# A two-layer decoder trunk: rounded halves for layer 0's gate, one weight chunk and 24 scalings between engines, first sums in pairs, and a new list of the order

## The chip, the cores and the metric

The kernel runs on one core of a Trainium2 chip, in one launch. The metric is the device time in microseconds. The five engines that the profile names are PE (TensorE), DVE (VectorE), ACT (ScalarE), POOL (GpSimd) and SP (SyncE, which here only asks for transfers).

## The reference, cut to what matters

Two layers act on 256 tokens of width 1024. Each normalises, scales and shifts by a conditioning vector, mixes, and adds the gated result. Layer 0 ("even") runs sliding-window attention with sinks (8 heads) beside a three-branch sparse attention (8 heads); layer 1 ("odd") runs block-sparse attention with 16 heads.

```python
def reference(x, c, w_ada, b_ada, norm_g, w_in_even, ...):
    c_act = jax.nn.silu(c)
    for layer in range(2):
        ada = jnp.einsum('bd,de->be', c_act, w_ada[layer]) + b_ada[layer]
        shift, scale, gate = jnp.split(ada, 3, axis=-1)      # 1024 each
        h = rms_norm(x, norm_g[layer]) * (1.0 + scale[:, None, :]) + shift[:, None, :]
        y = even_mixer(h, ...) if layer == 0 else odd_mixer(h, ...)
        x = x + gate[:, None, :] * y
    return rms_norm(x, final_g)

def even_mixer(h, w_in, w_out, ...):
    proj = jnp.einsum('bsd,de->bse', h, w_in)
    ...
    oa = swa_sink_attention(qa, ka, va, sinks, cos, sin) * jax.nn.silu(za)
    ob = nsa_attention(...) * jax.nn.silu(zb)
    return jnp.einsum('bse,ed->bsd', jnp.concatenate([oa, ob], axis=-1), w_out)
```

The products of activations and weights are wanted in float32 precision.

## The kernel before, in words

**Recording and issuing.** The program does not call the engines. A `Plan` records each operation with a number in order of recording and the numbers that it depends on; the line that finally calls an engine is line 244 for all of them, which is why the profile names L244 everywhere and why its rows are told apart by tiles. `issue()` emits the operations in the order of a literal list, `ORDER` (lines 37 to 154), in which every operation must stand behind those it depends on. Each engine executes its own operations in that order, so a wait of one holds up all behind it on its engine. SP's queue asks for the transfers in list order too.

**Float32 as rounded halves.** A matmul of float32 takes two passes in the trace. Projections therefore split both sides: `split` has ScalarE round a tile (`whi<-raw`, the CAST) and VectorE subtract (`wlo<-raw,whi`), and `mm3` multiplies hi x hi, hi x lo, lo x hi. `hhi`/`hlo` are the two halves of the layer's input, `ghi`/`glo` those of the gated mixer output. There are five `raw` buffers for weights, four `whi` and four `wlo`.

**The start.** x (`xs`) is loaded and normalised while layer 0's shift and scale columns arrive. These are sums over the 1024 rows of `w_ada`, weighted by silu(c) (`cz`). `START` (line 24) gives four groups (columns per group in blocks of 128, and `d`, how many of the eight row blocks VectorE sums itself). `first_ada` (691) asks for the first group's shift and scale columns in five transfers to `qT` and `gate`; `start_ada` asks for the later groups, and `start_row` (759) for the projection's weight rows. `start_sums` (714) sums with narrow matmuls of 32 columns of the array, four column groups q at a time (q = 0, 1 are shift, q = 2, 3 scale for two-block groups), copies the result (`asb<-ps_m`), transposes it, and adds the bias into `shs`. `start_prep` makes `hhi`/`hlo` from `bigA` and `shs`; `start_mm` accumulates the projection row block by row block. Warm-up matmuls (`ps_o<-ones`) fill the time before.

**The even layer.** `attn_four` (573) handles two pairs of heads: scores, one reduction with masks, an Exp with a sum, a reciprocal `rc`, a scaling of each probability tile by `rc` (128x128 for t=0, 128x256 for t=1), transposes and copies. `ON_ACT` (line 30) names the scalings that ScalarE does; the others are VectorE's. The tiles lie in `late` and `bigA`. It is called six times.

**Conditioning sums between.** `jobs` (1072) holds what is filled in between attention steps: layer 0's gate, then layer 1's shift and scale in two halves g=0 and g=4. `ada_wide` loads two row blocks at a time into `raw`; VectorE accumulates them into `acc` (one instruction of 128x1024 per row block). `SS_PE` (line 27) says how many of the four such chunks TensorE sums instead, straight from `raw`, in `ada_shift_scale`: for each row block four matmuls of 32 columns by 256. `ada_gate` (463) sums `acc` over the partitions with a matrix of ones; `GATE_R` (line 25) says for which layer it splits `acc` into rounded halves first (`whi<-acc`, `wlo<-acc,whi`) instead of multiplying in float32.

**Between the layers and at the end.** `out_proj` multiplies by `w_out`; `add_scaled` (378) multiplies by the gate, adds to `xs` and takes sums of squares into `parts`; GpSimd raises them to the power -0.5; then the rows are normalised, transposed and shifted into layer 1's `hhi`/`hlo`. The end of layer 1 does the same with the final norm; `LAST` (line 29) cuts the output into pieces for ScalarE ("a"), VectorE ("v") and a fused one ("f"), each with a transfer of its own.

Of the kernel before, what the change touches and what calls it, by code (L numbers as in the profile page):

```python
# [24 lines left out]
GATE_R = (0, 1)  # L25
HV = 4
SS_PE = {0: 0, 4: 2}
SPL = (1024, 1024, 512, 512)
LAST = ((("a", 0, 384), ("v", 384, 1024)), (("a", 0, 192), ("a", 192, 384), ("f", 768, 1024), ("v", 384, 768)))
ON_ACT = ((0, 0, 1), (0, 1, 1), (1, 0, 1), (1, 1, 1))  # L30
# [225 lines left out]
def tile_trunk(  # L256
# [23 lines left out]
    plan = Plan(tc.nc)  # L280
# [433 lines left out]
    def start_sums(g, n, d, w):  # L714
# [9 lines left out]
        terms = []  # L724
# [7 lines left out]
        ids = []  # L732
# [11 lines left out]
        for o in range(0, len(ids), 4):  # L744
            plan.group(ids[o : o + 4])
# [640 lines left out]
```

## Time and profile before

| | before |
|---|---|
| time, median of three runs | 294.93 us (294.6 to 295.61) |
| profiled execution, time | 295.04 us |
| profiled execution, span | 293.3 us |
| granted TensorE clock, mean | 0.995 |
| busy: TensorE, VectorE, ScalarE, GpSimd | 285.4, 252.8, 188.5, 8.1 us |
| moved by DMA | 71.72 MB |

The span runs from the first to the last instruction; the execution's own time is 1.74 us longer. In rows of instructions the first number is the start in us from the beginning of the span, the second the duration in us; then come the engine, the operation, output and inputs by the program's names, shape, and a count where equal neighbours are put together. In rows of groups, "x24 | 30.6, 1276" means 24 instructions, 30.6 us together, 1276 ns each. A bracket shows how long the engine was idle before and what ended that.

### The profile page before, as it was taken

Reading aid. Unit: us, or ns where it says so; the run is one execution under the profiler, and the core shown is the slowest. Engines: PE = TensorE matmul, PEld = TensorE weight load, DVE = VectorE, ACT = ScalarE, POOL = GpSimd, SP = SyncE. Lnnn points to the kernel's source line nnn. Section 1 sums busy time; section 2 is a strip of 40 time slices with the busy share of each in tenths; the row PEclk is TensorE's granted clock in tenths of the full one; section 3 lists DMA queues with packets and bytes.
Section 4 is the critical chain, followed back from the end, with each engine's and each line's share of the span. In section 5 each row is a group of like instructions: output and inputs, shape, how many; then the busy total and the mean of one; then the engine's idle time right before and its main releaser. Section 6 shows DMA issues by size and latency. Waiting matters only on the chain.

```text
span 293.3 us, 6197 instructions
## 1 busy us (share of the span) xinstructions
PE 285.4 (97%) x2293; PEld 246.6 (84%) x2293; DVE 252.8 (86%) x629; ACT 188.5 (64%) x480; POOL 8.1 (3%) x33
## 2 busy tenths in 40 slices
PE   8999999999999999999999999999999999999991
PEld 8888788897897888777767899998899999887891
DVE  0497797999999999999889759779978999899884
ACT  4456256895998899994457863366658368584531
POOL 3000000000000000000020000000000000000021
PEclk9999999999999999999999999999999999999998
DMA  7999999999969942769986954569489709502003
GB/s 262 381 365 380 384 380 349 344 349 322 389 233 359 351 147 74 249 234 332 333 256 206 349 167 135 191 242 283 146 258 291 244 0 335 205 36 72 1 3 142
DMA packets 48431, 71.72 MB, mean 245 GB/s; under 512 B 2490, under 2 KB 33938, under 8 KB 48402
## 3 DMA queue, kind: packets, MB, share of 16 engines
q1 hardware_dynamic: 47906, 70.93, 70.6%
q8 instruction: 18, 0.29, 0.4%
q10 hardware_dynamic: 496, 0.41, 0.4%
q14 instruction: 11, 0.09, 0.1%
HBM read 70.28 MB, written 1.05 MB: 243 GB/s over the span
## 4 chain that ended last, share of the span: by engine, by line
PE 82%; DMA 11%; DVE 1%; ACT 1%; issue 1%; POOL 1%; POOLq 0%; DVEq 0%; ACTq 0%
PE ps_pj L244 53%; PE ps_s L244 10%; PE ps_o L244 7%; PE ps_pt L244 7%; PE ps_m L244 5%; DMA gate<-in_w_ada_dram 3%; DMA late<-in_w_ada_dram 3%; DMA raw<-in_w_in_even_dram 3%; DMA qT<-in_w_ada_dram 2%; DMA xs<-in_x_dram 1%; DVE wlo L244 1%; ACT t L244 1%; ACT whi L244 1%; POOL parts L244 1%; DVE t L244 0%
## 5 line engine op out<-in xcount | busy, mean ns | idle before, releaser
L244 ACT CAST whi<-raw 128x512 fp32r<-128x512 f32 (+2 forms) x116 | 71.8, 658 | 27.1 <-PE ps_pj L244 16.5
L244 DVE TENSOR_TENSOR wlo<-raw,whi 128x512 fp32r<-128x512 f32 (+2 forms) x100 | 71.3, 740 | 7.3 <-ACT whi L244 6.6
L244 PE MATMUL ps_pj<-hlo,whi 128*128 128x256 f32 x256 | 70.0, 288 | 0.0
L244 PE MATMUL ps_pj<-hhi,whi 128*128 128x256 f32 x256 | 69.9, 289 | 0.0
L244 PE MATMUL ps_pj<-hhi,wlo 128*128 128x256 f32 x256 | 68.3, 284 | 0.0
L244 PEld LDWEIGHTS ps_pj<-hhi,whi 128*128 128x128 f32 x256 | 46.7, 188 | 1.6 <-issue 0.7
L244 PEld LDWEIGHTS ps_pj<-hlo,whi 128*128 128x128 f32 x256 | 47.1, 189 | 0.8 <-issue 0.7
L244 PEld LDWEIGHTS ps_pj<-hhi,wlo 128*128 128x128 f32 x256 | 46.7, 189 | 0.3
L244 ACT ACTIVATE late<-late,mn 128x128 f32<-128x128 f32 (+1 forms) x58 | 26.0, 450 | 9.2 <-DVE mn L244 9.1
L244 DVE SCALAR_TENSOR_TENSOR acc<-raw,cz,acc 128x1024 f32<-128x1024 f32 x24 | 30.6, 1276 | 0.1
L244 PE MATMUL ps_pj<-whi,hlo 128*128 128x512 f32 (+2 forms) x72 | 25.6, 373 | 0.0
L244 PE MATMUL ps_pj<-wlo,hhi 128*128 128x512 f32 (+2 forms) x72 | 25.5, 372 | 0.0
L244 DVE SCALAR_TENSOR_TENSOR wlo<-raw,whi 128x512 fp32r<-128x512 f32 x32 | 21.1, 686 | 4.5 <-ACT whi L244 4.4
L244 PE MATMUL ps_pj<-whi,hhi 128*128 128x512 f32 (+2 forms) x72 | 24.8, 373 | 0.0
L244 PE MATMUL ps_pj<-wlo,ghi 128*128 128x512 f32 (+1 forms) x56 | 20.6, 371 | 0.0
L244 PE MATMUL ps_pj<-whi,ghi 128*128 128x512 f32 (+1 forms) x56 | 20.6, 371 | 0.0
L244 PE MATMUL ps_pj<-whi,glo 128*128 128x512 f32 (+1 forms) x56 | 20.4, 367 | 0.0
L244 PE MATMUL ps_pt<-ta,late 128*128 128x128 f32 x87 | 19.6, 275 | 0.0
L244 ACT COPY late<-ps_pt 128x384 f32<-128x384 f32 (+1 forms) x29 | 14.0, 483 | 7.9 <-PE ps_pt L244 7.6
L244 PEld LDWEIGHTS ps_pj<-whi,hhi 128*128 128x128 f32 x72 | 13.4, 188 | 2.5 <-ACT hhi L244 0.7
L244 PEld LDWEIGHTS ps_pj<-whi,hlo 128*128 128x128 f32 x72 | 13.6, 188 | 2.0 <-issue 0.2
L244 PEld LDWEIGHTS ps_pj<-wlo,hhi 128*128 128x128 f32 x72 | 13.4, 189 | 1.6
(243 smaller groups left out, 591.0 us busy)
## 6 DMA issues: line engine op xcount, KB each, us to landing
raw<-in_w_in_odd_dram SPq DMA_DIRECT2D x16, 1024.0 KB, 5.7
raw<-in_w_ada_dram SPq DMA_DIRECT2D x8, 1024.0 KB, 8.3
raw<-in_w_ada_dram SPq DMA_DIRECT2D x16, 512.0 KB, 6.3
raw<-in_w_in_even_dram SPq DMA_DIRECT2D x5, 1024.0 KB, 7.9
raw<-in_w_in_even_dram SPq DMA_DIRECT2D x7, 652.0 KB, 7.6
late<-in_w_ada_dram SPq DMA_DIRECT2D x16, 256.0 KB, 6.8
raw<-in_w_out_even_dram SPq DMA_DIRECT2D x4, 1024.0 KB, 5.8
raw<-in_w_out_odd_dram SPq DMA_DIRECT2D x4, 1024.0 KB, 8.7
```

The source lines that it names most:

```text
L244: self.ops.append(dict(key=eng.key, deps=deps, fn=lambda: getattr(real, name)(*args, **kw)))
```

## The change

Four small edits and a new order:

1. `GATE_R`: layer 0's gate is summed in rounded halves too. Two float32 matmuls become four of rounded numbers, and a cast on ScalarE and a subtraction on VectorE of 128x1024 are added.
2. `SS_PE`: in the second half of layer 1's shift and scale, TensorE sums one chunk from `raw` instead of two. Eight matmuls go; VectorE gets two accumulations of 128x1024.
3. `ON_ACT`: all eight scalings of an `attn_four` call are ScalarE's; the four of t=0, 24 in all, leave VectorE.
4. `start_sums`: in the first group (`d` = 0) the column groups are issued two at a time, so the shift's sums and the scale's are separate bursts.
5. `ORDER`: a new list for the whole kernel, with 3000 numbers instead of 3002. In it the queue of SP asks, behind x, for scale 87 and 88, shift 85, scale 89, shift 86, then for row 91 (before: 85, 86, 87, 88, 89, 90). On TensorE the first sums of the scale half come first.

```diff
-GATE_R = (0, 1)
+GATE_R = (1, 1)
...
-SS_PE = {0: 0, 4: 2}
+SS_PE = {0: 0, 4: 1}
...
-ON_ACT = ((0, 0, 1), (0, 1, 1), (1, 0, 1), (1, 1, 1))
+ON_ACT = tuple((n, i, t) for n in range(2) for i in range(2) for t in range(2))
...
 ORDER = [int(i) for i in """
...
         ids = []
-        for m in range(max(len(tq) for tq in terms)):
-            for q, tq in enumerate(terms):
-                if m < len(tq):
+        size = 4 if d else 2
+        for o in range(0, 4, size):
+            for m in range(max(len(tq) for tq in terms)):
+                for q in range(o, o + size):
+                    tq = terms[q]
+                    if m >= len(tq):
+                        continue
                     ids.append(T.matmul(
...
-        for o in range(0, len(ids), 4):
-            plan.group(ids[o : o + 4])
+        for o in range(0, len(ids), size):
+            plan.group(ids[o : o + size])
```

Of the new order the prediction uses these places. On ScalarE, the cast of row 0's columns 512 to 1024 (`whi<-raw`) stands ahead of the first `asb<-ps_m` copy; before, behind it. On VectorE, between the layers, one subtraction `wlo<-raw,whi` moves from behind the normalised row of tokens 0 to 127 to ahead of it, and the add to `xs` of tokens 128 to 255 moves ahead of both `t<-ps_pj,shs` pieces. At the end, the 128x640 output scaling of tokens 0 to 127 moves behind the last reduction. The small transfers of the second layer's rows are asked for earlier, the gate's bias later.

232 rows, old and new, of the table ORDER are left out of this document.

## The prediction

> **What bounds the kernel now.** I read the page's totals, its slices and its chain first, to see which engine sets the end.
>
> ```profile
> span 293.3 us, 6197 instructions
> PE 285.4 (97%) x2293; PEld 246.6 (84%) x2293; DVE 252.8 (86%) x629; ACT 188.5 (64%) x480; POOL 8.1 (3%) x33
> ...
> PE   8999999999999999999999999999999999999991
> ...
> GB/s 262 381 365 380 384 380 349 344 349 322 389 233 359 351 147 74 249 234 332 333 256 206 349 167 135 191 242 283 146 258 291 244 0 335 205 36 72 1 3 142
> ...
> PE 82%; DMA 11%; DVE 1%; ACT 1%; issue 1%; POOL 1%; POOLq 0%; DVEq 0%; ACTq 0%
> ```
>
> TensorE is busy for 285.4 of 293.3 us, and 82% of the chain that ended last is its matmuls. The 11% of DMA is the start; the chain's longest pieces and TensorE's list of waits say where it lies.
>
> ```profile
> 4.16 7.62 DMA gate<-in_w_ada_dram
> 11.79 7.51 DMA late<-in_w_ada_dram
> 19.32 7.42 DMA raw<-in_w_in_even_dram
> 26.75 6.09 DMA qT<-in_w_ada_dram
> ...
> PE ps_m L244 <- DMA qT<-in_w_ada_dram: 0.5, 1, 0.5
> ```
>
> From 4.16 to 32.84 us the transfers lead: the first matmuls of the projection run as fast as rows and layer 0's shift/scale columns land. At about 32.8 us TensorE waits 0.5 us for the last of them, and nowhere later does that list name a wait. So behind 33 us a microsecond is gained only by taking work from TensorE, and lost by whatever makes it wait; ahead of 33 us a short delay of TensorE costs nothing as long as the transfers end no later. The third region is the tail behind the last matmul, where the last sums, the final norm and the output's transfers stand in a row.
>
> VectorE and ScalarE over the even layer's attention, in the windows from 70 to 140 and from 100 to 130 us (columns: window, length, PE, PEld, DVE, ACT, POOL, clock, DMA share, GB/s):
>
> ```profile
> 70.00:140.00 70.00, 70.00 (x605) 55.69 (x601) 69.03 (x217) 60.16 (x180) 0.00 (x0) 1.00 0.76 266
> 100.00:130.00 30.00, 30.00 (x226) 23.19 (x224) 29.89 (x95) 28.30 (x80) 0.00 (x0) 1.00 0.52 177
> ```
>
> VectorE is full (69.03 of 70) and TensorE still does not wait for it. ScalarE has 9.84 us free over the whole, but only 1.70 in the middle 30.
>
> **Part 1, layer 0's gate in rounded halves.** The two sums over partitions and their neighbours on TensorE, and the same job as layer 1 does it already:
>
> ```profile
> 100.85 1.02 PE L244 MATMUL ps_m<-acc,ones 128*128 128x512 f32 x2
> 101.80 1.08 PE L244 MATMUL ps_o<-bigA,vb 128*64 128x256 f32 x9
> ...
> 103.74 1.02 PE L244 MATMUL ps_m<-acc,ones 128*128 128x512 f32 x2
> 104.70 0.71 PE L244 MATMUL ps_s<-late,qT 64*128 64x128 f32 x6
> ...
> L244 ACT CAST whi<-acc x1: 1049/1049/1049, 247.4 to 247.4; 128x1024 fp32r<-128x1024 f32 x1
> L244 DVE TENSOR_TENSOR wlo<-acc,whi x1: 1218/1218/1218, 248.6 to 248.6; 128x1024 fp32r<-128x1024 f32 x1
> ...
> 149.16 0.40 PE L244 MATMUL ps_s<-whi,ghi 128*128 128x512 f32 x1
> ...
> 149.63 0.40 PE L244 MATMUL ps_s<-whi,glo 128*128 128x512 f32 x1
> ```
>
> From start to start the old sums hold TensorE 0.95 + 0.96 = 1.91 us. A matmul of rounded numbers of the same width starts 0.235 us after the last (149.16 to 149.63 is two steps), so the four new ones take 0.94. **Gain 0.97 us**, all on the path. The price is 1.05 us of ScalarE and 1.22 of VectorE ahead of the sums; the gate is read by the output projection's adds (one stands at 151.02 below), so its longer way alone delays nobody. What is queued behind the two instructions matters, and comes under part 3.
>
> **Part 2, one weight chunk of layer 1's shift and scale from TensorE to VectorE.** The sums lie between the layers, and so does the chain that they fill:
>
> ```profile
> 150.42 0.69 DVE L244 TENSOR_TENSOR wlo<-raw,whi 128x512 fp32r<-128x512 f32 x1
> 151.02 0.68 DVE L244 TENSOR_TENSOR t<-ps_s,gate 128x512 f32<-128x512 f32 x1
> 151.71 1.91 PE L244 MATMUL ps_m<-raw,cz 128*32 128x256 f32 x32
> 152.54 0.40 DVE L244 TENSOR_SCALAR t<-ps_pj,shs 128x128 f32<-128x128 f32 x1
> 153.03 0.41 ACT L244 CAST hhi<-t 128x256 fp32r<-128x256 f32 x1 [1.26 <-DVE t L244]
> 153.55 0.50 PE L244 MATMUL ps_pj<-whi,hhi 128*128 128x512 f32 x1
> ...
> L244 DVE SCALAR_TENSOR_TENSOR acc<-raw,cz,acc 128x1024 f32<-128x1024 f32 x24 | 30.6, 1276 | 0.1
> ```
>
> The 32 quarter matmuls hold TensorE from 151.71 to 153.55, 1.84 us; half of them go, 0.92 us. But they were filler: the next matmul reads the cast that ends at 153.44, so at the old timing the gap would simply show. What moves the cast is VectorE's new order. The subtraction that stood at 150.42, ahead of t=1's multiply by the gate, now stands ahead of the normalised row, in a stretch where VectorE waits for GpSimd's power. The multiply can then start when its bank is complete, at about 150.75 instead of 151.02; the two h pieces and the cast come as much sooner, though the add is now ahead of both of them. I therefore take **0.27 of 0.92 as gained** (ends: 0 and 0.92). The VectorE price is 2 x 1.28 = 2.55 us, somewhere before 140 us.
>
> **Part 3, 24 scalings from VectorE to ScalarE.** The t=0 pieces and their nearest kin on ScalarE (first rows: minimum/median/maximum in ns between 70 and 140 us):
>
> ```profile
> L244 DVE TENSOR_SCALAR late<-late,rc x15: 254/279/281, 75.1 to 128.3; 128x128 f32<-128x128 f32 x15
> L244 DVE TENSOR_SCALAR bigA<-bigA,rc x9: 274/279/286, 92.9 to 132.6; 128x128 f32<-128x128 f32 x9
> ...
> L244 ACT ACTIVATE late<-late,mn 128x128 f32<-128x128 f32 x29 | 11.5, 396 | 3.5 <-DVE mn L244 3.5
> ...
> L244 ACT CAST whi<-raw 128x512 fp32r<-128x512 f32 x92 | 53.3, 619 | 22.2 <-PE ps_pj L244 14.2 <-issue 3.2 <-DMA raw<-in_w_in_even_dram 2.5
> ...
> 150.65 1.12 ACT L244 CAST whi<-raw 128x512 fp32r<-128x512 f32 x2
> ```
>
> VectorE loses 24 x 0.279 = 6.7 us and gets 1.22 + 2.55 = 3.8, so it goes from 69.03 to 66.1 of 70. ScalarE pays at most 0.396 each, as for an Exp of this shape (9.5 us); two casts in a row take 1.12 where two alone take 1.24, so in a train the price is about 0.28 (6.7). With the gate's cast ScalarE stands at 67.9 to 70.7 of 70 us. Relief of VectorE buys nothing, since TensorE waits for it nowhere here. On ScalarE the weight casts and the copies of transposed probabilities, both read by TensorE, queue behind each added scaling. Cover is the slack that VectorE had while equally full: TensorE did not wait then. I take nothing for it; the ends are 0 and the price of the first rival.
>
> The Trainium skill, "ScalarE: Activation LUTs", section "What ACT_TABLE_LOAD costs", gives an ACTIVATE with one pointer operand 280 ns + 0.833 ns per column and takes off about 93 ns back to back: by that an estimate of 294 ns for each, 7.1 us in all, and ScalarE at 68.3 of 70. That is the lower end of the two above; the trace's 1.12 us for two casts agrees with an overlap.
>
> **Part 4, the first sums in pairs, and the new first transfers.** The start of the projection:
>
> ```profile
> 11.05 1.18 PE L244 MATMUL ps_m<-qT,cz 128*32 128x128 f32 x34
> ...
> 13.10 0.27 ACT L244 COPY asb<-ps_m 128x128 f32<-128x128 f32 x1 [3.83 <-PE ps_m L244]
> 13.26 0.62 ACT L244 CAST whi<-raw 128x512 fp32r<-128x512 f32 x1
> 14.74 0.47 PE L244 MATMUL ps_s<-whi,hhi 128*128 128x512 f32 x1
> ```
>
> Two column groups at a time instead of four let a quarter's sums start when its half has landed, at up to twice the PE time of these 64 instructions; they run while TensorE waits for rows, so I cost the pairs at nothing (up to 1.2 us if that cover were gone, the length of the burst at 11.05 once more). The new list asks the queue for the scale half's chunks first, with the shift half between them. On ScalarE it also puts a weight cast of row 0 ahead of the copy `asb`, whose row is asked for behind all ada chunks: the copy then starts after landing and cast, about 0.4 us later, and so does the first matmul. The same bytes end the start at about 32.8 us, and the 0.5 us wait there absorbs 0.4. The tiny row transfers, asked for earlier, add a few KB to that queue, and the gate's bias, asked later, is needed only with the gate's sums. **Start 0** (ends: -0.5, that wait gone, and +1.2).
>
> **Part 5, the tail.** Order on VectorE and the output's transfers:
>
> ```profile
> 285.84 0.55 DVE L244 TENSOR_SCALAR t<-xs,parts 128x640 f32<-128x640 f32 x1
> 286.43 3.81 SPq L244 DMA_DIRECT2D out_dram<-t  x3
> 288.38 0.55 POOL L244 TENSOR_TENSOR parts<-parts,expo 128x1 f32<-128x1 f32 x1 [1.93 <-DVE parts L244]
> 288.96 0.42 DVE L244 TENSOR_SCALAR t<-xs,parts 128x384 f32<-128x384 f32 x1 [0.67 <-POOL parts L244]
> ```
>
> The 128x640 scaling of tokens 0 to 127 stands at 285.84 and its 320 KB are asked for at 286.43, ahead of the last 512 KB. In the new order it stands behind the last reduction, in the 0.67 us in which VectorE waits for GpSimd's power: no VectorE time is lost on the path (0.55 fits in 0.67), but the 320 KB are asked for at about 288.9 and share the way with the last 512 KB. At the 380 GB/s of the best slices of the start they alone take 0.84 us; I take **+0.5** (ends 0 and +0.9), since about half fits into the stretch before the last pieces are asked for.
>
> **The rest of the list.** Most of each engine's order changes; a common order holds only 1248 of TensorE's 1910 instructions, 245 of VectorE's 545 and 179 of ScalarE's 398. Reordering takes no TensorE time by itself; I cost it at 0, with -0.5 to +1.5 as ends.
>
> **Sum.** 295.04 us (the profiled execution; 0.11 above the median of the runs, 294.93) - 0.97 - 0.27 + 0 + 0.5 = 294.30, or 294.2 against the median. I write 294.2. What a measurement here can tell from no change is 0.3%, 0.88 us, so this is within it, near its lower edge.
>
> **Rivals.** *ScalarE becomes the bound (slower).* Place: 100 to 130 us, where 13 of the 24 scalings lay (10 on `late`, 3 on `bigA`, with the rest around them). 28.30 + 13 x 0.28 to 0.40 + 1.05 is 33.0 to 34.6 in 30 us, so 3.0 to 4.6 us of casts must have been moved out. If half of that becomes TensorE's wait it is +1.5 to +2.3: 295.7 to 296.5. It decides from about 1.6 us of wait. For it: ScalarE at 28.30 of 30 already. Against: VectorE stood at 29.89 and nobody waited. *All TensorE time is kept (faster).* The chain between the layers gives way by the whole 0.92, and the tail's transfer is hidden: 295.04 - 0.97 - 0.92 = 293.15, and 292.65 if the wait at 32.8 us goes too. For it: every edit takes from a full engine. Against: the cast at 153.03. *Nothing comes of it:* the gate's saving meets a late operand soon after, the shift/scale saving is lost, the tail takes the rest: 294.9. *The start is uncovered:* sums in pairs at twice the time and the late cast delay everything, +1.2 on the forecast: 295.4 and up.
>
> **How the numbers follow.** Forecast 0.36 (a third of it beyond 0.88 us faster), all kept 0.25, ScalarE 0.24, nothing 0.10, start 0.05 (three fifths of it slower). So faster 0.25 + 0.12 = 0.37, same 0.24 + 0.10 + 0.02 = 0.36, slower 0.24 + 0.03 = 0.27. The forecast's own range is 293.6 to 294.9; the whole one, 292.6 to 296.3, leaves out the far ends of the first two rivals, about 0.2.
>
> **What would show it.** TensorE's busy time down by near 1.9 us; four matmuls of the gate 0.235 apart; TensorE's list of waits with an entry for the cast between the layers of 0.4 to 0.7 us (0 for the second rival) and none for ScalarE between 70 and 140 us (the first rival: over 1.5 us there); the first projection matmul near 15.1 us; the last matmul 1.2 us earlier and the tail behind it 0.5 us longer. The prediction is wrong if TensorE stands still anywhere else behind 33 us.

## The result: slower by 3.2 us, and the profile after

| | before | after |
|---|---|---|
| median of the runs (four each) | 294.88 us (294.6 to 295.61) | 298.06 us (297.8 to 298.43) |
| profiled execution | 295.04 us | 298.43 us |
| span, granted clock | 293.3 us, 0.995 | 296.7 us, 0.994 |

The ratio after to before is 1.0105 (95% interval 1.0082 to 1.0128). In this and the runs below, two executions that lie far outside all others (566 us in new_cast, 1586 us of the kernel before) are left out. The forecast was 294.2 with a range to 296.3: the time lies outside, past the upper end of the first rival too (296.5).

The page of after: totals, TensorE's slices, the chain's shares; then TensorE's list of waits (us in total, times, longest).

```profile
span 296.7 us, 6148 instructions
PE 286.3 (96%) x2277; PEld 247.4 (83%) x2277; DVE 251.7 (85%) x608; ACT 194.9 (66%) x505; POOL 9.1 (3%) x33
...
PE   8999999999999998999999999999999999999990
...
PE 63%; DVE 17%; DMA 10%; ACT 4%; issue 3%; POOL 1%; POOLq 0%; DVEq 0%; ACTq 0%; SPq 0%
```

```profile
PE ps_pt L244 <- ACT t L244: 1.0, 1, 1.0
PE ps_pj L244 <- ACT hhi L244: 0.5, 1, 0.5
PE ps_pt L244 <- ACT hhi L244: 0.4, 1, 0.4
PE ps_pj L244 <- DVE t L244: 0.3, 1, 0.3
```

The chunk's sixteen records are gone from TensorE (2293 to 2277) and the gate's four hold it for 1.36 us instead of 1.91, and yet it is busy 0.9 us longer. A TensorE without gaps reads as busy whatever it does: this row measures the length of the span and not the work. The chain tells more: TensorE's part fell from 82% to 63%, and 17% are now VectorE's. The wait for the start's last transfer (0.5 us) is gone, and four waits for other engines have come.

To place the rest, each matmul's time from its start to the start of the next was added up by place, after minus before:

| place | after - before, us |
|---|---|
| start, to 60 us | +1.08 |
| 60 to 110 us, in small pieces | +0.56 |
| the gate's sums | -0.55 |
| one stop at 111.9 us | +1.16 |
| rest of 110 to 150 us | +0.11 |
| between the layers: 0.86 removed, 0.96 come back | +0.10 |
| 160 us to the last matmul (+0.84 in 220 to 240, -0.57 in 240 to 260) | +0.20 |
| behind the last matmul's start | +0.72 |
| sum (the spans differ by 296.70 - 293.33 = 3.37) | +3.38 |

**The start.** Rows of after's timeline from 12.7 us on:

```profile
12.73 0.83 PE L244 MATMUL ps_m<-qT,cz 128*32 128x128 f32 x12
...
12.97 0.62 ACT L244 CAST whi<-raw 128x512 fp32r<-128x512 f32 x1
...
14.69 0.27 ACT L244 COPY asb<-ps_m 128x128 f32<-128x128 f32 x1 [1.10 <-PE ps_m L244]
...
16.29 0.73 PE L244 MATMUL ps_pj<-whi,hhi 128*128 128x512 f32 x2
```

The cast ends at 13.59 and the copy still stands 1.10 us for TensorE's sums. TensorE has no gap between 9.62 and 15.9 us: it is the sums in pairs that are late (12 of them in 0.83 us, where the burst before took 1.18 for 34). The 64 sums hold TensorE for 3.35 us in four bursts, before for 1.88 in one, and transposes and warm-up matmuls stand between the bursts. The first projection matmul starts at 16.29 instead of 14.74. The prediction had 15.1, with the cast as the cause.

**The stop at 111.9 us.** SP's queue, VectorE's subtraction, then ScalarE and TensorE, from four stretches of after's timeline (the queue's durations are its issuing); behind them the same two requests before, and four pieces of after's chain:

```profile
85.88 0.99 SPq L244 DMA_DIRECT2D raw<-in_w_in_even_dram  x1
...
96.07 1.22 DVE L244 TENSOR_TENSOR wlo<-raw,whi 128x1024 fp32r<-128x1024 f32 x1
...
97.35 0.37 SPq L244 DMA_DIRECT2D raw<-in_w_ada_dram  x1
...
100.29 3.95 SPq L244 DMA_DIRECT2D raw<-in_w_out_even_dram  x2
...
111.40 1.05 ACT L244 CAST whi<-raw 128x1024 fp32r<-128x1024 f32 x1 [1.59 <-DMA raw<-in_w_out_even_dram]
...
112.36 0.40 ACT L244 ACTIVATE bigA<-bigA,rc 128x128 f32<-128x128 f32 x1
...
112.66 0.46 ACT L244 COPY t<-ps_pt 128x384 f32<-128x384 f32 x1
...
113.17 0.33 PE L244 MATMUL ps_pt<-ta,late 128*128 128x128 f32 x1 [0.99 <-ACT t L244]
```

```profile
98.33 4.18 SPq L244 DMA_DIRECT2D raw<-in_w_out_even_dram  x2
```

```profile
73.31 8.82 DMA raw<-in_w_ada_dram
...
101.57 2.27 DVE wlo L244 x2
103.87 7.51 DMA raw<-in_w_out_even_dram
111.40 1.05 ACT whi L244
```

Read from the end: TensorE waits 0.99 us for ScalarE's copy that frees `ps_pt`. The copy stands behind a scaling of 0.40, and both behind a cast before which ScalarE stood idle for 1.59 us, since its weights had not landed. The two requests for that matrix stand at 100.29 and 103.87, before at 98.33 and 102.14. Ahead of them SP asks for nothing between 85.88 and 97.35, since the next buffer comes free with the subtraction that ends at 97.29; the request of 103.87, whose landing releases the cast, follows another subtraction. So from 73 to 111 us the chain that ended last runs through transfers and VectorE's work on the buffers, where before it was TensorE's own. The windows of 90 to 100 us, before and then after, show the hole in the transfers (the last two columns):

```profile
90.00:100.00 10.00, 10.00 (x94) 9.01 (x93) 10.00 (x24) 8.79 (x26) 0.00 (x0) 1.00 1.05 361
```

```profile
90.00:100.00 10.00, 10.00 (x96) 8.69 (x89) 9.93 (x33) 9.99 (x29) 0.00 (x0) 1.00 0.32 99
```

**Between the layers.** After's timeline, and the power before:

```profile
152.23 0.69 DVE L244 TENSOR_TENSOR wlo<-raw,whi 128x512 fp32r<-128x512 f32 x1
...
152.25 1.09 POOL L244 TENSOR_TENSOR parts<-parts,expo 128x1 f32<-128x1 f32 x1 [2.36 <-DVE parts L244]
...
155.92 0.41 ACT L244 CAST hhi<-t 128x256 fp32r<-128x256 f32 x1 [0.79 <-DVE t L244]
...
156.37 0.50 PE L244 MATMUL ps_pj<-whi,hhi 128*128 128x512 f32 x1 [0.47 <-ACT hhi L244]
```

```profile
149.43 0.55 POOL L244 TENSOR_TENSOR parts<-parts,expo 128x1 f32<-128x1 f32 x1 [0.93 <-DVE shs L244]
```

The subtraction did move into the gap in which VectorE waits for GpSimd's power. But the power, which took 0.55 us before, takes 1.09 beside it, so the row that the subtraction should no longer delay comes 0.5 us later anyway.

**The tail**, after:

```profile
289.43 0.27 PE L244 MATMUL ps_pj<-whi,glo 128*128 128x256 f32 x1
...
290.71 0.55 DVE L244 TENSOR_SCALAR t<-xs,parts 128x640 f32<-128x640 f32 x1
290.88 0.79 POOL L244 TENSOR_TENSOR parts<-parts,expo 128x1 f32<-128x1 f32 x1 [1.07 <-DVE parts L244]
291.29 1.76 SPq L244 DMA_DIRECT2D out_dram<-t  x3
```

The same again: the scaling stands in the gap, and the power beside it takes 0.79 instead of 0.55. The 320 KB are asked for at 291.29, before at 286.43. ScalarE's 128x384 piece of the same tokens is late too: its request stands at 290.48, before at 285.09. From the last matmul's start to the end there are 7.27 us, before 6.55: 0.09 more up to the end of the power, which begins sooner behind that matmul than before, and 0.63 more behind it.

### The profile page after: what moved, and what is told of

The parts are those of the page before. It is cut to its first block, busy times and chain, and to the rows that moved or that the text cites. A ratio compares the mean times of both kernels' runs of the same rounds, so it can differ in the third digit from the quotient of the medians.

```text
span 296.7 us, 6148 instructions
## 1 busy us (share of the span) xinstructions
PE 286.3 (96%) x2277; PEld 247.4 (83%) x2277; DVE 251.7 (85%) x608; ACT 194.9 (66%) x505; POOL 9.1 (3%) x33
## 3 DMA queue, kind: packets, MB, share of 16 engines
HBM read 70.28 MB, written 1.05 MB: 240 GB/s over the span
## 4 chain that ended last, share of the span: by engine, by line
PE 63%; DVE 17%; DMA 10%; ACT 4%; issue 3%; POOL 1%; POOLq 0%; DVEq 0%; ACTq 0%; SPq 0%
PE ps_pj L244 40%; PE ps_o L244 8%; PE ps_s L244 6%; PE ps_pt L244 5%; DVE wlo L244 5%; DVE acc L244 3%; PE ps_m L244 3%; DMA raw<-in_w_ada_dram 3%; DVE t L244 3%; DMA raw<-in_w_out_even_dram 3%; DMA late<-in_w_ada_dram 2%; DMA raw<-in_w_in_even_dram 2%; ACT whi L244 2%; DVE xs L244 2%; DVE oT L244 1%
## 5 line engine op out<-in xcount | busy, mean ns | idle before, releaser
L244 PE MATMUL ps_pj<-hlo,whi 128*128 128x256 f32 x256 | 69.1, 288 | 0.0
L244 DVE SCALAR_TENSOR_TENSOR acc<-raw,cz,acc 128x1024 f32<-128x1024 f32 x26 | 33.2, 1278 | 0.5 <-DMA raw<-in_w_ada_dram 0.4
L244 ACT ACTIVATE late<-late,mn 128x256 f32<-128x256 f32 (+1 forms) x58 | 25.9, 450 | 6.6 <-DVE mn L244 6.6
L244 PE MATMUL ps_pj<-whi,hhi 128*128 128x512 f32 (+2 forms) x72 | 26.0, 379 | 0.6 <-ACT hhi L244 0.5
L244 PE MATMUL ps_pt<-ta,late 128*128 128x128 f32 x87 | 20.2, 275 | 1.1 <-ACT t L244 1.0
L244 ACT ACTIVATE whi<-raw 128x512 fp32r<-128x512 f32 x16 | 9.8, 629 | 10.2 <-PE ps_pj L244 6.3
```

Source lines behind the costliest of these rows:

```text
L244: self.ops.append(dict(key=eng.key, deps=deps, fn=lambda: getattr(real, name)(*args, **kw)))
```

## The experiments

The theories at the start: the first rival of the prediction (ScalarE's added scalings delay TensorE), and against it that the new list's places cost the time, each at another spot ("the order", O). Later a third: that VectorE and ScalarE together have more to do than the order can hide ("the amount", W). Kernels named old_ start from the kernel before, those named new_ from the changed one. All times are medians; the ratio is to the kernel before on the same chip, with its interval.

### All edits in the old list, and three repairs of the new one

**old_all**: edits 1 to 4, old list, the new instructions put in where their inputs are ready; the gate's halves are made 512 columns at a time, in a part of `ghi`/`glo` that is free then.

```diff
+GATE_R = (1, 1); SS_PE = {0: 0, 4: 1}; ON_ACT = all eight; sums in pairs
 ORDER = (the old list; 24 scalings at their places, on ScalarE)
```

> All four edits, but in the old list: new operations are put where their inputs are ready, the rest keeps its place (the gate's halves are made 512 columns at a time, in a buffer that is free there). Theory L (the new list loses the time): the edits keep most of their gain here, TensorE's busy time falls by about 1.8 us and the time is 293.2 to 294.8 us; no ScalarE wait over 0.5 us between 70 and 140 us. Theory S (24 scalings fill ScalarE whatever the list): TensorE waits 1 to 2 us for ScalarE between 70 and 140 us and the time is 295.5 to 297 us.

Measured: 304.31 us, ratio 1.0331 (1.0282 to 1.038). TensorE waits 2.7 us for `ghi` at 146.5 us and 1.5 us for VectorE at 104, more than either theory had. With the edits the new list is 6.2 us better than the old one as filled in here.

**new_noact**: edit 3 undone, list unchanged.

```diff
-ON_ACT = tuple((n, i, t) for n in range(2) for i in range(2) for t in range(2))
+ON_ACT = ((0, 0, 1), (0, 1, 1), (1, 0, 1), (1, 1, 1))
```

> The new kernel with the 24 scalings back on VectorE, same list. Theory S (ScalarE too full): the 1.16 us wait at 111.9 us goes, and with it 1.5 to 2.5 us of the time: 295.6 to 296.6 us. Theory L (the list's places): ScalarE still stops 1 to 1.6 us for the weights of the output projection at about 111 us, since that transfer lands no sooner, and the time stays within 0.8 us: 297.3 to 298.4 us.

Measured: 300.71 us, 1.0177 (1.0149 to 1.0204). TensorE's list of waits now begins

```profile
PE ps_pt L244 <- DVE late L244: 1.5, 3, 0.9
```

Taking the scalings off ScalarE makes the kernel 2.6 us slower: the wait for ScalarE's copy shrinks from 1.0 to 0.2 us, but VectorE is late three times instead. (The traced execution took 302.07 us.) So giving them to ScalarE is not what costs the time in this list.

**new_fours**: edit 4 undone, at the same places of the list.

```diff
-        size = 4 if d else 2
-        for o in range(0, 4, size):
+        for m in range(max(len(tq) for tq in terms)):
+            for q, tq in enumerate(terms):
```

> The new kernel with the first sums four column groups at a time again, at the same places of the list. If the pairs' TensorE time is what delays the first projection matmul (16.3 us): it starts at 14.9 to 15.5. If the transfers of the start's weight rows then set the end (theory D): the time falls by 0 to 0.5 us only, because a wait comes back at 32 or at 48 us: 297.5 to 298.1. If not (theory P): the whole 1 to 1.5 us come back: 296.5 to 297.1 us.

Measured: 298.94 us, 1.0131 (1.0116 to 1.0146). The start of TensorE's timeline:

```profile
10.34 0.43 PE L244 MATMUL ps_m<-qT,cz 128*32 128x128 f32 x8 [0.57 <-DMA qT<-in_w_ada_dram]
...
12.45 0.41 PE L244 MATMUL ps_m<-qT,cz 128*32 128x128 f32 x4 [0.73 <-DMA qT<-in_w_ada_dram]
...
17.09 0.73 PE L244 MATMUL ps_pj<-whi,hhi 128*128 128x512 f32 x2
```

Four at a time need both halves at once, and in the new order of transfers the halves come interleaved. So in the new list the pairs help by 0.9 us; they are slow, and waiting is slower.

**new_gaps**: the subtraction behind the normalised row again, and the tail's instructions in their old order.

```diff
-... 1584 1593 1656 1585 1586 1595 1594 ...
+... 1584 1593 1585 1586 1595 1594 1656 ...
```

> The new kernel with two places of the list as in the old one: between the layers the subtraction stands behind the normalised row again, so VectorE is idle while GpSimd takes the power; in the tail everything but TensorE has the old order, so the 128x640 scaling and its transfer come early. Theory G (VectorE at work stretches GpSimd's power): the power between the layers goes from 1.09 to about 0.55 us, TensorE's waits there fall by 0.4 to 0.9, the tail by 0.5 to 0.8: 296.4 to 297.1 us. Rival (the powers' spans are only rough, the waits have another cause): between the layers nothing changes, and the time is 297.3 to 298.1 us.

Measured: 297.72 us, 1.009 (1.0075 to 1.0105); 0.3 better than after. Its timeline:

```profile
152.13 0.56 POOL L244 TENSOR_TENSOR parts<-parts,expo 128x1 f32<-128x1 f32 x1 [2.36 <-DVE parts L244]
...
155.87 0.41 ACT L244 CAST hhi<-t 128x256 fp32r<-128x256 f32 x1 [1.40 <-DVE t L244]
...
156.32 0.50 PE L244 MATMUL ps_pj<-whi,hhi 128*128 128x512 f32 x1 [0.88 <-ACT hhi L244]
```

The power is back at 0.56, so the subtraction did stretch it. The cast `hhi` does not come sooner, since the subtraction now delays the multiply by the gate and so the add in front of the h pieces: from the start of the output projection's last matmul to the first of layer 1 it is 3.76 us, 3.69 in after and 3.22 before. Either place of that one instruction costs the same in this list; the gain that remains is the tail's (6.56 us; 6.55 before).

### Single edits in the old list, the late cast, the old start

**new_cast**: the cast for which ScalarE stood at 111.4 us goes behind the copy that frees `ps_pt`.

```diff
-... 1280 1245 1437 1246 ... 1276 1253 1123 1254 ...
+... 1280 1245 1246 ... 1276 1253 1123 1437 1254 ...
```

> The new kernel with one instruction of ScalarE's list moved: the first cast of the output projection's weights, which waits for its transfer at 111 us, stands behind the copy of transposed probabilities instead of ahead of it (its subtraction on VectorE follows it). Theory C (a cast that waits for its transfer holds the copy that TensorE needs): the wait of 1.0 us for ScalarE at 112 us falls to under 0.4, the time by 0.5 to 1.1: 296.9 to 297.6 us. Rival (the wait only moves to the next cast or to the output projection): 297.8 to 298.4 us.

Measured: 298.29 us (three executions), 1.0114 (1.0097 to 1.0131). The trace of this kernel is shown under new_cast2, below.

**new_start**: the start in the old order, with the groups of four.

```diff
 ORDER = (to the end of the start: the old list's relative order, pairs undone)
```

> The new kernel with the whole start (everything recorded before the second row transfers, up to about 50 us, all engines and SP) in the old relative order, and the first sums four at a time; the rest in the new order. If the start costs what the matched matmuls say (about 0.7 to 1.1 us by 50 us): 296.9 to 297.5 us, first projection matmul at 14.7, wait at 32 us back, none at 48 us. Rival (the start is set by the transfers either way): 297.8 to 298.4 us.

Measured: 308.78 us, 1.0463 (1.0445 to 1.048). TensorE waits 8.0 us from 47.0 us on for small row transfers, which are now asked for late while their transposes stayed early. This says what such a mismatch costs and nothing on the start itself; new_start2 mends it.

**old_gate**: edit 1 alone, old list, halves as in old_all.

```diff
-GATE_R = (0, 1)
+GATE_R = (1, 1)
```

> The old kernel and list with layer 0's gate in rounded halves alone (made 512 columns at a time, right behind the last accumulation and behind the first sum). If its price on the other engines is hidden: 0.97 us less of TensorE, 293.8 to 294.3 us. Theory F (in the old list VectorE and ScalarE have no room here, and what is put in delays what TensorE needs): TensorE waits 1 to 3 us between 100 and 120 us, and the time is 295.3 to 297.5 us.

**old_act**: edit 3 alone, each scaling at its old place in the list.

```diff
-ON_ACT = ((0, 0, 1), (0, 1, 1), (1, 0, 1), (1, 1, 1))
+ON_ACT = tuple((n, i, t) for n in range(2) for i in range(2) for t in range(2))
```

> The old kernel and list with the 24 scalings on ScalarE alone, each at its old place of the list. Theory S (ScalarE at 98 to 101% between 70 and 140 us): TensorE waits for ScalarE's copies and casts, 1.5 to 4 us in all: 296.5 to 299 us. Theory N (the share between two full engines does not matter while nobody waits): 294.5 to 295.5 us.

Measured: old_gate 298.85 us, 1.0125 (1.0102 to 1.0149); old_act 298.48, 1.0117 (1.0102 to 1.0132). The first new waits of the one and of the other:

```profile
PE ps_pt L245 <- DVE t L245: 1.5, 1, 1.5
...
PE ps_pt L245 <- ACT bigA L245: 1.0, 1, 1.0
```

```profile
PE ps_pt L244 <- ACT t L244: 1.4, 2, 1.1
```

Each of the two by itself costs about as much in the old list as all the edits do in the new one. What part 1 saves on TensorE's sums is lost several times over to waits behind what VectorE and ScalarE have queued.

### The start, the layer boundary and the gaps, each by itself

**new_start2**: new_start with the small row transfers at their new places.

```diff
 ORDER = (as new_start; the row transfers stay where the new list has them)
```

> The new kernel with everything recorded up to the last projection matmul of the start in the old relative order, four column groups at a time; the small row transfers and all the rest stay at their new places. If the start costs what the matched matmuls say: first projection matmul near 14.7 us, no wait at 48 us, 296.9 to 297.5 us. Rival (the delay of the start is taken up later, by transfers or by ScalarE at 112 us): 297.7 to 298.4 us.

Measured: 300.05 us, 1.0177 (1.0156 to 1.0198). The first projection matmul is at 14.18 us and the wait at 48 is gone, but new ones stand between 44 and 57 us (0.6 for `wlo`, and smaller ones); the wait for ScalarE's copy, now at 114, is still 0.9. In this try the late start of after was no loss that could be taken out alone.

**old_pairs**: edit 4 alone.

```diff
-        for m in range(max(len(tq) for tq in terms)):
-            for q, tq in enumerate(terms):
+        size = 4 if d else 2
+        for o in range(0, 4, size):
```

> The old kernel and list with the first sums in pairs alone. If TensorE has room while it waits for rows (the prediction's cover): first projection matmul at 14.7 to 15.0 us and 294.8 to 295.3 us. If it has none: first projection matmul 1.0 to 1.6 us later, of which the wait at 32 us gives 0.6 back: 295.4 to 296.2 us.

Measured: 295.0 us, 1.0003 (0.9994 to 1.0013): nothing. TensorE's timeline:

```profile
10.97 1.08 PE L244 MATMUL ps_m<-qT,cz 128*32 128x128 f32 x32 [0.40 <-DMA qT<-in_w_ada_dram]
...
14.78 0.70 PE L244 MATMUL ps_s<-whi,hhi 128*128 128x512 f32 x2
```

The sums wait for rows (0.40 us), and the first projection matmul stays at 14.78. But this run does not test the cover: its list puts a pair of the shift beside a pair of the scale, and TensorE takes the two together, 32 sums in 1.08 us where before took 1.18 for 34. Sums at twice the time were not tried in the old order.

**new_bt**: the boundary and the tail in their old relative order.

```diff
 ORDER = (between the layers and behind them: the old list's relative order)
```

> The new kernel with the stretch between the layers (from layer 0's output projection to layer 1's first projection, all engines) and the tail in the old relative order. Theory G (the order of TensorE there and VectorE beside GpSimd's power cost about 1 us, the tail 0.4 to 0.7): TensorE's wait for the first odd cast falls from 1.0 in sum to under 0.5, the time to 296.4 to 297.1 us. Rival (the wait is the filler that is gone): the wait stays, 297.4 to 297.9 us.

Measured: 302.74 us, 1.0266 (1.0223 to 1.0308): waits of 1.7 us for `wlo` at 160.8, 0.8 for `late` at 131.1, 0.8 for `hhi`. The old order here does not fit the new one ahead of it.

**old_gaps**: the kernel before with only the two moves into the gaps of the power: the subtraction one place up, the 128x640 scaling behind the last reduction.

```diff
-... 1587 1596 1656 1597 ...          ... 2936 2983 ... 2987 2937 2988 ... 2992 2993
+... 1587 1656 1596 1597 ...          ... 2983 ... 2987 2988 ... 2992 2936 2937 2993
```

> The old kernel with three instructions moved and nothing else: the subtraction between the layers ahead of the normalised row, into GpSimd's power, and in the tail the 128x640 scaling with its transfer behind the last reduction. Theory G: the power between the layers goes from 0.55 to about 1.1 us, the last power from 0.55 to about 0.8, the transfer meets the last ones: 0.6 to 1.3 us more, 295.6 to 296.4 us. The prediction's view (the gap is free, the transfer costs 0.5): 0.2 to 0.5 more, 295.2 to 295.6 us.

Measured: 295.57 us, 1.002 (1.0011 to 1.0029): slower by 0.6. Both powers in its timeline:

```profile
149.01 1.01 POOL L244 TENSOR_TENSOR parts<-parts,expo 128x1 f32<-128x1 f32 x1 [0.93 <-DVE shs L244]
...
288.02 0.79 POOL L244 TENSOR_TENSOR parts<-parts,expo 128x1 f32<-128x1 f32 x1 [1.69 <-DVE parts L244]
```

0.55 to 1.01 and 0.55 to 0.79: this is the one part of the change whose loss stands by itself, free of the list. In the trace, from the start of the output projection's last matmul to the first of layer 1 it is 3.67 us (before 3.22), and from the last matmul's start to the end 6.83 (before 6.55). (The traced execution took 295.17 us; it has no wait for the start's last transfer.) The trace of before had a row that showed it, a power beside the two-input add `xs<-xs,bigA`, which I had not read:

```profile
283.48 0.93 POOL L244 TENSOR_TENSOR parts<-parts,expo 128x1 f32<-128x1 f32 x1 [0.93 <-DVE parts L244]
```

The Trainium skill, "GPSIMD Engine Reference", section "8. Key points", says that GpSimd shares its memory interfaces with VectorE and that they contend when a VectorE instruction has two inputs in SBUF or runs in a two-port mode; the subtraction has two such inputs, and the trace agrees (0.55 to 1.01).

### The amount of work, and part 2 alone

**new_noscale** and **old_noscale** leave out the 24 scalings of t=0 altogether, in after and in the kernel before: these probabilities stay undivided.

```diff
+                    if t == 0:
+                        pass
-                    if (n, i, t) in ON_ACT:
+                    elif (n, i, t) in ON_ACT:
```

> The new kernel with the 24 moved scalings left out altogether (the probabilities of t=0 stay unscaled), everything else in place. Theory W (ScalarE and VectorE carry more work than the stretch from 60 to 150 us holds): ScalarE gets 6.7 to 9.5 us free there, TensorE's wait at 112 us goes, and the time falls by 1.5 to 3 us: 295 to 296.5. Theory O (single places of the order): the cast at 111 us still waits for its transfer, and the time falls by under 0.8 us: 297.3 to 298.1.

> The old kernel with the same 24 scalings left out (VectorE loses 6.7 us between 70 and 140 us, TensorE and ScalarE keep their work). If TensorE waits for nobody there, as its list of waits said: 294.7 to 295.2 us, no change. If small waits for VectorE are hidden between matmuls: 293.5 to 294.5 us.

Measured: new_noscale 299.32 us, 1.0165 (1.0127 to 1.0203); old_noscale 295.0, 1.001 (0.9998 to 1.0021). Between 60 and 140 us ScalarE of new_noscale is busy 66.6 us instead of 74.5 in after and 67.9 before, and the kernel is 1.3 us slower than after. The amount (W) falls, as far as one list can say it. Where the time went, in its timeline (an execution of 301.57 us):

```profile
128.70 1.04 ACT L243 CAST whi<-raw 128x1024 fp32r<-128x1024 f32 x1 [2.11 <-DMA raw<-in_w_out_even_dram]
129.78 1.23 DVE L243 TENSOR_TENSOR wlo<-raw,whi 128x1024 fp32r<-128x1024 f32 x1 [2.04 <-ACT whi L243]
129.80 0.73 PE L243 MATMUL ps_s<-whi,ghi 128*128 128x512 f32 x2 [1.33 <-ACT whi L243]
```

Again a cast that stands for a weight transfer. old_noscale says that VectorE's relief buys nothing, as the prediction had it.

**new_nostt** leaves out the two accumulations that part 2 gave to VectorE: one chunk of layer 1's shift and scale is missing from its sums.

```diff
-        if u < 0 or u >= 4 - on_pe:
+        if u < 0 or u >= 4 - on_pe or (l == 1 and c0 == 512 and u == 2):
```

> The new kernel without the two accumulations that came to VectorE (that chunk of layer 1's shift and scale is left out). Theory W: VectorE gets 2.55 us free before the layers' boundary, the time falls by 0.5 to 1.5 us: 296.5 to 297.5. Theory O: under 0.4 us: 297.7 to 298.2.

**old_ss**: part 2 alone; the chunk's second transfer is asked for right behind its first, and the accumulations stand between the adds of the first output half.

```diff
-SS_PE = {0: 0, 4: 2}
+SS_PE = {0: 0, 4: 1}
```

> The old kernel and list with the shift/scale chunk on VectorE alone (its second transfer asked for behind the first, the two accumulations put between the adds of the first output half). If the filler is simply gone and the accumulations cost nothing: 294.4 to 295.1 us. If they delay the adds and the weight subtractions that the boundary needs: 1 to 2.6 us more, 296 to 297.5 us.

Measured: new_nostt 298.59 us, 1.0116 (1.0093 to 1.0139), no gain over after; old_ss 298.45, 1.012 (1.0105 to 1.0135). In old_ss two accumulations in front of a subtraction stop TensorE for 1.92 us. Its TensorE timeline, and the window of the microsecond from 149:

```profile
147.45 0.50 PE L244 MATMUL ps_s<-wlo,ghi 128*128 128x512 f32 x1 [1.92 <-DVE wlo L244]
...
149.03 0.63 PE L244 MATMUL ps_s<-whi,ghi 128*128 128x512 f32 x1
149.46 0.63 PE L244 MATMUL ps_s<-wlo,ghi 128*128 128x512 f32 x1
```

```profile
149.00:150.00 1.00, 1.00 (x4) 0.77 (x3) 0.97 (x3) 0.67 (x3) 0.00 (x0) 0.50 0.87 198
```

A second loss follows the stop: the granted clock is 0.92 at 148, 0.50 from 149 to 152 and 0.87 at 152, and matmuls that start 0.23 us apart before it start 0.43 apart.

### The repairs together

**new_cast2**: new_cast once more, for its trace.

```diff
 (as new_cast)
```

> The kernel of new_cast once more, for its trace. Its time did not move (298.6 against 298.1). Theory C': the wait at 112 us falls to under 0.4 us, and the same time comes back as a wait behind it, for the next weights or for the output projection's halves. Rival: the copy waited for something else, and the wait at 112 us is still 0.9 to 1.2 us.

**new_gc**: new_gaps and new_cast in one kernel.

```diff
 (the diffs of new_gaps and of new_cast)
```

> The new kernel with both the places of new_gaps and the moved cast of new_cast. If each place of the order costs by itself, the two add up to new_gaps: 297.5 to 298.1 us. If the wait at 112 us moves to the boundary between the layers and new_gaps makes room there: 296.6 to 297.3 us.

Measured: new_cast2 298.07 us, 1.011 (1.0081 to 1.0139); new_gc 297.49, 1.0077 (1.0046 to 1.0108). The timeline of new_cast2:

```profile
110.48 0.48 ACT L244 COPY t<-ps_pt 128x384 f32<-128x384 f32 x1 [0.83 <-PE ps_pt L244]
...
114.47 0.33 PE L244 MATMUL ps_pt<-ta,late 128*128 128x128 f32 x1 [0.53 <-ACT late L244]
```

The copy comes at 110.48 instead of 112.66 and the stop at 112 is gone, which shows that the waiting cast made it; 0.53 us comes back at 114.47, where TensorE waits for a scaling of `late` that stands a few instructions behind that same cast. In time the seven executions of this kernel (297.1, the one of the trace, to 299.09) cannot be told from after's, so the stop's 1.16 us is no saving to be had by this move alone. new_gc, the best version of the changed kernel, is 0.6 us better than after and still slower than the kernel before. No version beat the kernel before.

## Why the prediction was wrong, point by point

- **The step that failed: "The rest of the list ... I cost it at 0".** Its ends were -0.5 to +1.5. The list brought the stop at 111.9 us (+1.16) and the small losses from 60 to 110 (+0.56). I argued that reordering takes no TensorE time, and did not follow the one queue that the order moves too: SP's. Its requests for the output projection's weights came about 2 us later, where a cast had no slack, and behind a hole of 11.5 us.
- **Part 4 and the start, taken as 0:** +1.08 to 60 us. The price was in the prediction (1.2 us "if that cover were gone"), and so was the rival that names it, at a chance of 0.05. The cover was read from before's trace, with its transfers in another order. After does not have it: its 64 sums take 3.35 us instead of 1.88, without a gap on TensorE. Whether the old order would have had it no run shows, since old_pairs issues its pairs side by side. It ought to have been asked anew for the new order. Of the wait at 32.8 us I was right that it would go (-0.65); a new one at 48 us (0.40 for `hhi`, behind a cast that stood 1.05 for its transfer) took the place.
- **Part 1:** the matmuls' own gain is there, but 0.55 of 0.97. The last of the four holds its place for 0.59 instead of 0.235 us, because the next instruction waits for a scaling of `late` that ScalarE ends at 115.63 us, one of part 3's.
- **Part 2:** forecast -0.27, came out at +0.10. The placing was right (the gap shows, as a wait of 0.47 for the cast), the gain was not: the subtraction in the gap costs the power 0.54 us. I counted VectorE's time there and not GpSimd's. new_gaps gives the 0.54 back and gains nothing here, since the subtraction then delays the multiply: neither place shortens the chain that the removed sums had filled.
- **Part 3:** relief of VectorE buys nothing (old_noscale, 1.001): right. "I take nothing" for ScalarE's load holds inside the new list only in this sense: undoing it or leaving it out is slower. In the old list it costs 3.4 us. ScalarE's busy time between 60 and 140 us rose by 6.6 us with the gate's cast, where the sum had 7.7 to 10.5.
- **Part 5:** +0.5 forecast, +0.72 measured, 0.63 of it behind the power, where the forecast had put it. That the size came near is in part luck: the same move in the old list (old_gaps) costs 0.19 there, and in the new list ScalarE's 128x384 piece is asked for 5.4 us later as well. The power's 0.24 was not in the sum.
- **The first rival** named ScalarE and the region, and there TensorE waits 1.0 us for ScalarE: but for one that stands for a transfer, not one with too much to do. What its added scalings cost in the new list by themselves is the 0.35 us at the gate's last sum, under part 1.

The sum, by these terms: forecast -0.74 (-0.97 - 0.27 + 0.5). Start +1.08 and list +2.03 (0.56 + 1.16 + 0.11 + 0.20), gate +0.42 and boundary +0.37 short, tail +0.22 more: +4.12, together +3.38.

What is settled: the loss lies in several places, not in one instruction (the two repairs give 0.6 of 3.2), and leaving work out did not bring it back (less work was not faster, three times). How much of it the list alone would cost, without the edits, no run shows. Open are the small pieces from 60 to 110 us, for which no wait is listed, and the +0.84 and -0.57 from 220 to 260 us. Open is also whether some other list would make these edits pay: the placements tried in the old list were one for each.

## What to carry to other kernels

In a kernel whose engines follow one fixed order, an edit's price is its effect on that order: three edits that each save TensorE or VectorE some time cost 3.4 to 3.8 us apiece in the old list, at the one placement tried, and leaving work out won nothing. When the order is new, read every cover (who waits for what) in the new order, the transfer queue's first: for each cast of a weight, when its transfer is asked for and which buffer it waits for. An instruction put into a gap of one engine is not free if it slows the engine that makes the gap, as the power shows (0.55 to 1.09 us).

## What the runs showed of the hardware

- GpSimd's power of 128x1 takes 0.55 us alone, 1.01 to 1.09 beside a VectorE subtraction with two inputs in SBUF, 0.93 beside the two-input add, and 0.79 beside the 128x640 scaling with one. In each of these the power ends 0.41 or 0.42 us behind the end of that VectorE instruction (152.92 and 153.34 in after).
- Waits of TensorE of 1.33 us (new_noscale, to 129.80), 1.46 (old_all, to 105.51) and 1.92 (old_ss, to 147.45) were followed, about 1.4 us after work went on, by 3.4 us at half the granted clock, and the 8.0 us of new_start by 10.2 us of it. The wait of 0.99 us in after left it at 1.00, but so did 1.46 in old_gate (at 104), 1.70 in new_bt (at 161) and 2.74 in old_all (at 146.5): the length of the stop alone does not decide. The Trainium skill, "TensorE: Matmul & The Clock Gate", section "Part 1: The HAM clock gate", gives an idle window of about 3.4 us for that fall; the measurement differs, since stops of less than half of that were enough here.
- Narrow matmuls of 128x32 by 128 start in groups that follow each other 0.11 us apart, whether two column groups or four are in flight: 12 in pairs take 0.83 us from 12.73 on in after, 34 in fours 1.18 from 11.05 on before, with 0.27 us of the last one in each. So a matmul costs about 0.055 us in pairs and 0.028 in fours. In old_pairs, where a pair of the shift stands beside one of the scale, 32 take 1.08 us.
